# One encoder layer on one core: how the sums of squares reach memory, and when the last layer's stored products leave

## The chip, the cores and the metric

The kernel runs on one core of one Trainium2 chip, as one launch. The metric is the device time in microseconds (us) of that core, the median of several runs of the same program; lower is better. Beside the timed runs there is one profiled execution, from which all views of the trace come.

## The reference, cut to what matters

Two request groups (prompt and sample) of 2048 tokens with 1024 channels share one set of weights. For each group the layer computes, in float32:

```
h    = x * rsqrt(mean(x*x) + eps) * norm_w            # per token
proj = h @ w_in                                       # q_a k_a v_a g_a | q_b k_b v_b g_b
o_a  = windowed_gqa_sink(rope(rms(q_a)), rope(rms(k_a)), v_a) * silu(g_a)     # +-128 tokens
o_b  = neighbourhood_attn(rms(q_b), rms(k_b), v_b, rpb) * silu(g_b)           # 64-wide token grid
x    = x + concat(o_a, o_b) @ w_out
y    = x + (p @ w_ple) * sigmoid(x @ w_ple_gate)
```

Only one detail of it is touched by the first half of the change: `mean(x*x)` is needed once per token by group A, whose tiles hold 128 consecutive tokens, and again by group B, whose tiles hold 8 x 16 patches of the token grid. The second half touches how `p @ w_ple` is kept until the last line needs it.

## The kernel before, in words

Every product is split into three float32r products (high x high, high x low, low x high), so the matrix engine (PE) carries some three times the plain work. The work runs in four stages.

- **Group A**, 32 tiles of 128 tokens (16 for each of the two sequences), up to about 715 us. `proj_a(f)` projects tile f: 24 matmuls each for k and v (tile `pk`), for q (`pq`) and for the gate (`pg`). Two attention units per tile (`unit_a`, one for each key head) run between those matmuls.
- **Group B**, 64 tiles (two halves of the heads), up to about 1740 us, in the same manner (`proj_b`, `unit_b`).
- **The product p @ w_ple**, made by `ple_ahead(n)` for n = 0 to 7, eight blocks m of 6 matmuls each: PSUM tile `pple`, copied by ScalarE (ACT) into `ev` and stored by SyncE's DMA queue (SP) to `ple_d`. The first five n run beside the last units of group B, the last three alone (`tail=True`).
- **The two output products**, `product(m, mi)` into PSUM tiles `acca` and `accc`, with the operand pieces split by ACT (L1208) and VectorE (DVE, L1209).

What sets the order: all PE instructions are chained in the order in which the program emits them (`pinned`). `filler(f)` yields one projection matmul at a time, and the loop over f mixes these with the parts of the attention units at the shares of a tile that PLAN_A and PLAN_B give. A step marked `P` (keep_in_program_order) stays behind the instruction emitted before it on its own engine; unmarked ones are placed by the framework's scheduler. Every DMA that the change and its surroundings touch is issued by SP, in one queue, and runs on the same 16 DMA engines.

Buffers that matter: PSUM tag "ms" has two banks, shared by `pkt` (keys turned), `pqt` (queries turned), `po` (a unit's output, held until L741 has read it) and, in the last stage, the first two `acca`. Tag "pj" has three banks, shared by the projections, by `pple` and by later accumulators, the third and fourth `acca` among them. In SBUF, tag "s" has five buffers: in the last three `ple_ahead` they hold `ev`, so the copy of a block waits until the store of the block five before it has landed; after that they hold the results `r`.

The mean of squares of tile f is column f of `ms_a`, one number per partition, made early in the tile (L502) from the two squares of the token-major loads `stn` (L338, squared by ACT at L369). It is stored at L601 at the end of the tile. For group B `regroup(s)` lists, after the last tile of a sequence, sixteen gathers that read it back in the order of the patches (`regroup_next`, two per tile, L639) into `ms_b`.

In `ple_ahead`, `store_ple(1)` after the copy of block m issues the store of block m-1 (list `made`), so each store is queued one block late; the two extra calls `store_ple(1)` (after `drain(stream)` and after `drain(rest)`) issue the ones left over.

Of the kernel before, what the change touches and what calls it, by code (L numbers as in the profile page):

```python
# [11 lines left out]
F32 = mybir.dt.float32  # L12
# [5 lines left out]
SEQ = 2048  # L18
DM = 1024
NT = SEQ // 128  # L20
# [80 lines left out]
def emit(ctx, tc, io):  # L101
    nc = tc.nc
# [4 lines left out]
    def ptile(shape, tag, name):  # L107
        tag = PSM.get(tag, tag)
        return pp.tile(shape, F32, tag=tag, name=name, bufs=PSB[tag])
# [8 lines left out]
    ms_a = cp.tile([128, 2 * NT], F32, tag="ms_a", name="ms_a")  # L118
# [11 lines left out]
    ms_d = dram.tile([2 * SEQ], F32, tag="ms_d", name="ms_d")  # L130
# [28 lines left out]
    P = tc.keep_in_program_order  # L159
# [6 lines left out]
    def flush(key):  # L166
        pump(max((i + 1 for i, (k, _) in enumerate(jobs) if k == key), default=0))
# [72 lines left out]
    def pinned(ins):  # L240

        if last_pe:
            tc.add_manual_dep(ins.ins, last_pe.pop().name,
                              mybir.DependencyInfo(mybir.DependencyClass.NoSync, mybir.DependencyReason.DATA),
                              reason="tensor engine order")
        last_pe.append(ins.ins)
# [7 lines left out]
    def mm(out, lhsT, rhs, start, stop):  # L254
        pinned(nc.tensor.matmul(out, lhsT, rhs, start=start, stop=stop))  # L255

    def tr(out, in_, eye=ident):
        pinned(nc.tensor.transpose(out, in_, eye))  # L258
# [63 lines left out]
    ap = ab_stack.enter_context(tc.tile_pool(name="ab", bufs=1))  # L322
# [60 lines left out]
    ps = ptile([128, 512], "ms", "pwarm")  # L383
# [82 lines left out]
    for i in range(2):  # L466
        t = ap.tile([128, 2, 512], F32R, tag=f"q2{i}", name=f"q2{i}")
# [24 lines left out]
    def proj_a(f):  # L492
        s, t = divmod(f, NT)
# [68 lines left out]
        sq = ap.tile([128, 512], F32, tag="sq", name="sq", bufs=2)  # L562
# [35 lines left out]
        else:  # L598
            gate()
        held[f] = q, gs, y  # L600
        P(nc.sync.dma_start(ms_d[128 * f:128 * f + 128].rearrange("(p c) -> p c", c=1), ms))  # L601
        if t == NT - 1:
            regroup(s)
        else:
            regroup_next()
# [23 lines left out]
    def regroup(s):  # L629
        rows = ms_d.rearrange("(r k c) -> r k c", k=4, c=16)  # L630
        regroups.extend((ms_b[:, i:i + 1], rows[8 * (i // 4):8 * (i // 4) + 8, i % 4, :].rearrange("r c -> c r"))
                        for i in range(NT * s, NT * s + NT))
# [3 lines left out]
    def regroup_next():  # L636

        for dst, src in regroups[:2]:
            P(nc.sync.dma_start(dst, src))  # L639
        del regroups[:2]  # L640
# [293 lines left out]
    ple_d = [dram.tile([128, KT, TW], F32, tag=f"ple_d{n}", name=f"ple_d{n}") for n in range(len(tiles))]  # L934
    p_st, p_rs, early = {}, {}, {}

    def load_p(n):
        if n < len(tiles):
            s, u = tiles[n]
            p_st[n] = []  # L940
            for k in range(2):
                st = main.tile([128, TW], F32, tag="stage", name="p32", bufs=2)
                nc.sync.dma_start(st, io["p_t"][s][128 * k:128 * k + 128, TW * u:TW * u + TW])
                p_st[n].append(st)

    def split_p(n, later=False):

        t = p_rs[n] = main.tile([128, 2, 2, TW], F32R, tag="xr", name="p_r", bufs=2)

        def job(hi, lo, src):  # L950
            nc.scalar.copy(hi, src)
            nc.vector.tensor_tensor(out=lo, in0=src, in1=hi.bitcast(F32), op=ALU.subtract)
        for k, src in enumerate(p_st.pop(n)):
            todo = partial(job, t[:, k, 0], t[:, k, 1], src)
            if later:
                jobs.append((f"p{n}", todo))
            else:
                todo()
# [13 lines left out]
    def load_coming(n=1):  # L972

        for name, tag, key in coming[:n]:
            w = main.tile([128, 2, 512], F32R, tag=tag, name=tag, bufs=1)
            nc.sync.dma_start(w.bitcast(F32), parts_d[key])
            early[name].append(w)
        del coming[:n]

    made = []  # L980

    def store_ple(n):

        for dst, ev in made[:n]:
            nc.sync.dma_start(dst, ev)
        del made[:n]

    def ple_ahead(n, tail=False):

        load_p(n + 1)  # L990
        for m in range(KT):
            if m % 4 == 3 and (n < 3 or m == 3):
                load_coming()
            ps = ptile([128, TW], "pj", "pple")
            if m == 5 and n + 1 < len(tiles):
                split_p(n + 1)
            flush("p0")
            for k in range(2):
                w, c = early["p"][2 * (m // 4) + k], 128 * (m % 4)
                for i, (a, b) in enumerate(((0, 0), (0, 1), (1, 0))):  # L1000
                    mm(ps, w[:, a, c:c + 128], p_rs[n][:, k, b], k == 0 and i == 0, k == 1 and i == 2)
                    yield 215
            if tail:
                ev = main.tile([128, TW], F32, tag="s", name="ev", bufs=SB)
            else:
                ev = ap.tile([128, TW], F32, tag=("ev", "sq")[m // 2 % 2], name="ev", bufs=3 - m // 2 % 2)
            P(nc.scalar.copy(ev, ps))
            store_ple(1)
            made.append((ple_d[n][:, m], ev))

    qs = {}

# [4 lines left out]
    def filler(f):  # L1017

        gen = proj_a(f) if f < 2 * NT else proj_b(f)
        for n, (cost, last_one) in enumerate(gen):  # L1020
            if last_one:
                next(gen)
            elif hold[0] > 0:
                hold[0] -= 1
            elif n % step[0] == step[0] - 1:
                pump()
            yield cost

    def drain(gen, count=10 ** 9):
        for _ in range(count):  # L1030
            if next(gen, None) is None:
                return
# [16 lines left out]
    def paired(f, n):  # L1049
# [20 lines left out]
        else:  # L1070
            for name in ("a12", "a22"):
                load_early(name)
        w_b[half] = w

    stream = chain(*(paired(f, last[f]) if f in last else filler(f) for f in range(2, 6 * NT) if f - 1 not in last),
                   *(ple_ahead(n) for n in range(AHEAD)))
    drain(stream, 24)
    done = 2
# [32 lines left out]
                keys_b(*p)  # L1111
            owed = 16
    drain(stream)
    store_ple(1)


    ab_stack.close()
    with tc.tile_pool(name="c", bufs=1, reuse_waits="tile") as op:
# [171 lines left out]

        load_raw(0, 0)
        drain(ple_ahead(AHEAD, True))
        load_raw(0, 1)
        drain(ple_ahead(AHEAD + 1, True))
        for _ in range(4):
            load_x()
# [5 lines left out]
            piece(0, k)  # L1302
        load_q(0, "s2")
        drain(rest)
        store_ple(1)
        for _ in range(4):
            load_x()
        for name in ("s1", "s3", "s4"):
# [1 line left out]
        for m in range(7 * len(groups)):  # L1310
            n, i = divmod(m, 7)
# [92 lines left out]
```

## Time and profile before

| | |
|---|---|
| median of 3 runs | 2491.75 us (2488.02 to 2493.52) |
| the profiled execution | 2489.69 us, span of its instructions 2487.9 us |
| PE busy | 2459.3 us, 99% of the span |
| DVE / ACT / POOL (GpSimd) busy | 1702.9 / 1413.9 / 863.4 us |
| mean granted TensorE clock | 0.997 |
| DMA packets; under 512 B | 247140; 32400 |

How to read the views that follow. In a timeline or a group, a line names the start, the time taken, the engine, the line of the kernel, the operation, its output and input tiles, the count ("x6": six instructions merged), and in square brackets how long the engine stood idle before it and what released it. In a waits view the three numbers are total us, how often, and the longest. A line of the windows view gives, for a stretch of the span, its length, the busy time of each engine with the count of instructions, the granted clock of PE (PEclk, 1.00 is full), the busy share of the DMA engines, and GB/s. A busy PE is not PE at its peak: matmul ends are modelled, and a matmul at half clock counts as busy too.

### The profile page before, as it was taken

The page shows a single profiled execution, that of the slowest core. Times are in us where ns is not written, and L with a number is a line of the kernel's source. Part 1 is how long each engine was busy: PE and PEld are TensorE (multiplying, and loading weights), DVE is VectorE, ACT ScalarE, POOL GpSimd, SP SyncE. Part 2 cuts the span into 40 slices and gives each one's busy share as a digit, 9 for nine tenths or more (in the row PEclk, how much of TensorE's full clock was granted, in tenths as well). Part 3 has the DMA queues.
Part 4 walks back from the last instruction along what each step waited for, and adds up shares of the span by engine and source line. Part 5 has one row for each costly group of instructions (what it writes and reads, how often), then busy time and mean ns, then how long its engine had stood idle before and what let it go on. Part 6 is the DMA issues. An engine that isn't in the chain of part 4 may idle for free.

```text
span 2487.9 us, 40537 instructions
## 1 busy us (share of the span) xinstructions
PE 2459.3 (99%) x13048; PEld 2078.0 (84%) x13048; DVE 1702.9 (68%) x4210; ACT 1413.9 (57%) x3405; POOL 863.4 (35%) x1365
## 2 busy tenths in 40 slices
PE   9999999999999999999999999999999999999999
PEld 7888888888878888888788888888777888888887
DVE  6777777777765666666666666666536655687776
ACT  6777776777664665565656566666653222344443
POOL 5555555555444544544444444443100000000000
PEclk9999999999999999999999999999999999999999
DMA  7655554455374566555855566667876445756765
GB/s 204 143 111 96 98 88 102 96 92 98 82 195 137 167 190 183 169 167 184 288 171 184 177 205 210 199 198 239 295 255 233 161 169 175 267 171 219 243 227 169
DMA packets 247140, 438.87 MB, mean 176 GB/s; under 512 B 32400, under 2 KB 86800, under 8 KB 241680
## 3 DMA queue, kind: packets, MB, share of 16 engines
q1 hardware_dynamic: 246640, 436.27, 59.6%
q8 instruction: 104, 1.70, 0.3%
q14 instruction: 108, 0.88, 0.1%
q10 hardware_dynamic: 288, 0.01, 0.0%
HBM read 308.24 MB, written 133.19 MB: 177 GB/s over the span
## 4 chain that ended last, share of the span: by engine, by line
PE 91%; DMA 4%; DVE 3%; ACT 1%; issue 1%; POOL 0%; SPq 0%; ACTq 0%; DVEq 0%; POOLq 0%
PE pqk L255 14%; PE acca L1226 14%; PE pvg L255 14%; PE accc L1226 10%; PE pg L255 6%; PE pq L255 5%; PE scb L255 4%; PE ptb L258 3%; PE pob L255 3%; PE pple L255 3%; PE pk L255 3%; PE po L255 3%; PE sc L255 3%; PE pt L258 2%; DMA stn<-x_n 1%; DMA vw<-v_d 1%
## 5 line engine op out<-in xcount | busy, mean ns | idle before, releaser
L287 ACT ACTIVATE s<-s,nm 128x320 f32<-128x320 f32 (+6 forms) x512 | 294.4, 576 | 314.9 <-DVE nm L282 193.9
L255 PE MATMUL pvg<-wb,xr 128*128 128x512 f32 x1536 | 462.6, 408 | 1.3 <-DMA wb<-sp_0wb 0.6
L255 PE MATMUL pqk<-wa,xr 128*128 128x512 f32 x1536 | 442.9, 410 | 0.0
L255 PEld LDWEIGHTS pqk<-wa,xr 128*128 128x128 f32 x1536 | 266.1, 189 | 36.9
L255 PEld LDWEIGHTS pvg<-wb,xr 128*128 128x128 f32 x1536 | 266.7, 189 | 34.2 <-DMA wb<-sp_0wb 2.2
L1208 ACT CAST opd<-raw 128x512 fp32r<-128x512 f32 x224 | 131.5, 618 | 273.3 <-PE acca L1226 115.2
L356 POOL TENSOR_TENSOR xr<-stx,xr 128x512 fp32r<-128x512 f32 x188 | 241.6, 1295 | 106.3 <-ACT xr L355 84.0
L1209 DVE TENSOR_TENSOR opd<-raw,opd 128x512 fp32r<-128x512 f32 x224 | 146.4, 685 | 151.7 <-ACT opd L1208 151.7
L255 PE MATMUL pg<-wb,xr 128*128 128x512 f32 x768 | 233.5, 410 | 1.8 <-DVE vv L518 1.0
L255 PE MATMUL pq<-wa,xr 128*128 128x512 f32 x768 | 219.4, 400 | 0.0
L271 DVE CUSTOM_DVE_ANT_0 s<-scb,bias 128x288 f32<-128x288 f32 (+3 forms) x256 | 142.0, 555 | 104.6 <-PE scb L255 104.5
L137 POOL TENSOR_TENSOR yb<-vrb,power 128x8 f32<-128x8 f32 x64 | 106.5, 1664 | 236.1 <-DVE vrb L787 222.6
L1226 PE MATMUL accc<-opd,wb 128*128 128x512 f32 x768 | 176.7, 389 | 0.0
L1226 PE MATMUL acca<-opd,wa 128*128 128x512 f32 x768 | 176.6, 391 | 0.0
L1226 PE MATMUL acca<-opd,s 128*128 128x512 f32 x768 | 175.4, 389 | 0.0
L1226 PEld LDWEIGHTS acca<-opd,wa 128*128 128x128 f32 x768 | 145.1, 189 | 30.3
L1226 PEld LDWEIGHTS accc<-opd,wb 128*128 128x128 f32 x768 | 144.2, 188 | 29.9
L1226 PEld LDWEIGHTS acca<-opd,s 128*128 128x128 f32 x768 | 144.2, 188 | 29.9
L918 DVE TENSOR_TENSOR otb<-pob,otb 64x512 f32<-64x512 f32 x128 | 88.1, 689 | 112.8 <-ACT otb L917 111.2
L255 PEld LDWEIGHTS pob<-p_t,vw 128*128 128x128 f32 (+2 forms) x832 | 133.0, 189 | 27.6 <-DVE p_t L899 5.0
L255 PEld LDWEIGHTS pq<-wa,xr 128*128 128x128 f32 x768 | 135.1, 189 | 17.3
L715 DVE TENSOR_TENSOR pr<-pt,pr 128x512 fp32r<-128x512 f32 (+2 forms) x248 | 135.5, 549 | 16.5 <-ACT pr L713 13.2
(167 smaller groups left out, 5177.0 us busy)
## 6 DMA issues: line engine op xcount, KB each, us to landing
stx<-x_b SPq DMA_DIRECT2D x128, 256.0 KB
vw<-v_d SPq DMA_DIRECT2D x112, 256.0 KB
stx<-x_a SPq DMA_DIRECT2D x64, 256.0 KB
stn<-x_n SPq DMA_DIRECT2D x64, 256.0 KB
v_d<-vb SPq DMA_DIRECT2D x64, 256.0 KB
ple_d<-ev SPq DMA_DIRECT2D x64, 256.0 KB
xres<-x_r SPq DMA_DIRECT2D x64, 256.0 KB
x_d<-r SPq DMA_DIRECT2D x64, 256.0 KB
```

What stands on the lines that cost most here:

```text
L137: nc.gpsimd.tensor_tensor(out=y, in0=v, in1=power.broadcast_to([128, n]), op=ALU.pow)
L255: pinned(nc.tensor.matmul(out, lhsT, rhs, start=start, stop=stop))
L258: pinned(nc.tensor.transpose(out, in_, eye))
L271: nc.vector.tensor_tensor_reduce(out=s, in0=ps[:, :n], in1=bias, scale=1.0, scalar=-3.0e38, op0=ALU.add, op1=ALU.max, accum_out=sm["mx"][: ...
L287: ex = nc.scalar.activation(ss[i], ss[i], AF.Exp, bias=nm[:, i:i + 1], accum_out=den[:, i:i + 1])
L356: low.tensor_tensor(out=lo, in0=raw, in1=hi.bitcast(F32), op=ALU.subtract)
L715: nc.vector.tensor_tensor(out=pr[r, 1, to], in0=pt[r, c], in1=pr[r, 0, to].bitcast(F32), op=ALU.subtract)
L918: nc.vector.tensor_tensor(out=ot[a:a + 64], in0=pq[a:a + 64], in1=ot[a:a + 64], op=ALU.add)
L1208: P(nc.scalar.copy(hi, v))
L1209: P(nc.vector.tensor_tensor(out=lo, in0=v, in1=hi.bitcast(F32), op=ALU.subtract))
L1226: pinned(nc.tensor.matmul(ps, w[k][:, a, c:c + 128], o[:, b], start=i in (0, 1, 4) and k == 0 and j == 0, stop=k == 3 and j == 2, skip_gro ...
```

## The change

After it, tiles 0 to 14 and 16 to 30 store no sums. At the last tile of each sequence (t = 15, so f = 15 and f = 31) PE turns the sixteen columns of `ms_a` of that sequence into sixteen rows of 128 (PSUM tile `pms`, tag "ms"), ACT copies them into `row` (tag "sq"), and one DMA stores them as sixteen rows. The gathers of `regroup` stay as they are.

In the last three `ple_ahead` each block's store is issued right after its own copy. The two extra `store_ple(1)` calls are gone; the one store that is left over from n = 4 is issued by the call at the first block of n = 5.

```diff
@@ -598,8 +598,12 @@
         held[f] = q, gs, y
-        P(nc.sync.dma_start(ms_d[128 * f:128 * f + 128].rearrange("(p c) -> p c", c=1), ms))
         if t == NT - 1:
+            ps = ptile([128, 512], "ms", "pms")
+            tr(ps[:NT, :128], ms_a[:, NT * s:NT * s + NT])
+            row = ap.tile([128, 512], F32, tag="sq", name="row", bufs=2)
+            P(nc.scalar.copy(row[:NT, :128], ps[:NT, :128]))
+            P(nc.sync.dma_start(ms_d[s * SEQ:(s + 1) * SEQ].rearrange("(t p) -> t p", p=128), row[:NT, :128]))
             regroup(s)
         else:
             regroup_next()
@@ -1006,7 +1010,10 @@
             P(nc.scalar.copy(ev, ps))
             store_ple(1)
-            made.append((ple_d[n][:, m], ev))
+            if tail:
+                nc.sync.dma_start(ple_d[n][:, m], ev)
+            else:
+                made.append((ple_d[n][:, m], ev))
@@ -1111,7 +1118,6 @@
     drain(stream)
-    store_ple(1)
@@ -1302,7 +1308,6 @@
         drain(rest)
-        store_ple(1)
```

## The prediction

> **What bounds the kernel now.** I read the page first, then the waits of PE, then the timeline around its longest stalls, and last the DMA rate in the stretches that those led to.
>
> ```profile
> span 2487.9 us, 40537 instructions
> PE 2459.3 (99%) x13048; PEld 2078.0 (84%) x13048; DVE 1702.9 (68%) x4210; ACT 1413.9 (57%) x3405; POOL 863.4 (35%) x1365
> PE pple L255 <- ACT ev L1007: 5.7, 1, 5.7
> PE pt L258 <- DVE ot L742: 5.4, 2, 4.9
> PE pvg L255 <- DMA wb<-sp_0wb: 0.6, 2, 0.3
> ```
>
> PE is busy for 2459.3 of 2487.9 us: 28.6 us is idle, and no edit that leaves the matmuls alone can bring much more than that (plus what a slowed clock behind a stall costs). The first two rows of the waits are single stalls of 5.7 and 4.9 us, over a third of that idle time. So the question is whether the change touches one of them. It touches both.
>
> **The tail stall (the second half of the change).** Timeline around the last `ple_ahead`, SP, ACT and PE, then the chain and a windows row:
>
> ```profile
> 1853.29 3.30 SPq L1245 DMA_DIRECT2D xres<-x_r  x4
> 1856.64 0.43 SPq L1158 DMA_DIRECT2D raw<-oa_d  x1
> 1857.12 0.50 SPq L1160 DMA_DIRECT2D raw<-ob_d  x1
> 1857.72 2.05 SPq L985 DMA_DIRECT2D ple_d<-ev  x3
> 1859.82 4.80 SPq L1140 DMA_DIRECT2D s<-sums  x4
> 1866.83 6.61 SPq L985 DMA_DIRECT2D ple_d<-ev  x6
> 1853.41 0.59 ACT L1007 COPY ev<-pple 128x512 f32<-128x512 f32 x1 [0.55 <-PE pple L255]
> 1860.07 0.59 ACT L1007 COPY ev<-pple 128x512 f32<-128x512 f32 x1
> 1867.91 1.56 ACT L1007 COPY ev<-pple 128x512 f32<-128x512 f32 x3 [7.25 <-DMA ple_d<-ev]
> 1868.55 2.93 PE L255 MATMUL pple<-p_r,wa 128*128 128x512 f32 x6 [5.68 <-ACT ev L1007]
> 1871.28 12.08 PE L1226 MATMUL acca<-opd,wa 128*128 128x512 f32 x48
> L1226 PE MATMUL acca<-opd,wa 128*128 128x512 f32 x768 | 176.6, 391 | 0.0
> 1868.55:1871.48 2.93, 2.93 (x7) 2.35 (x8) 0.00 (x0) 0.93 (x2) 0.00 (x0) 0.50 1.05 401
> ```
>
> Read it backwards. PE's last six `pple` matmuls (n = 7, m = 7) waited 5.68 us for a PSUM bank: tag "pj" has three, and block 7 takes the one of block 4. Block 4's copy waited in ACT (7.25 us) for one of the five "s" buffers, the one whose store is that of the block five earlier, n = 6, m = 7. By the code that store is queued one block late, so SP reaches it only after the four residual loads and the two `raw` loads of 1 MB: it is the first of the three at 1857.72, although its copy, the one at 1853.41, was over by 1854.0. Behind 2 MB of reads it landed at about 1867.9, when the three waiting copies start.
>
> With the change that store goes out right behind its copy, ahead of the residual loads from 1853.29 and of the 2 MB. Block 4 is copied at about 1860.7, behind the copy at 1860.07, and block 7's matmuls start where PE stopped, 1868.55 - 5.68 = 1862.87. What is won: the 5.68 us, and the slow clock after it. A matmul of 512 columns takes 176.6/768 = 0.23 us; the six took 2.93 instead of 1.38, and the next 48 took 12.08 instead of 11.04, while the granted clock stood at 0.50: 2.6 us more. Together 8.3 us.
>
> The Trainium skill, in TensorE: Matmul & The Clock Gate, Part 1 (The HAM clock gate), says that about 3.4 us without work drops PE to half clock and about 3.4 us of work lifts it again. By that rule a long stall would cost 1.7 us extra where the rows here show 2.6; with 1.7 at both stalls the sum below would be 0.6 us smaller. The rows decide.
>
> What is late next in the tail: blocks 5, 6 and 7 of n = 7 now wait for the stores of blocks 0, 1 and 2, which stand behind the 2 MB as the three of 1857.72 did before, so their copies run from about 1867.9 to 1869.7. PE does not need them at once: block 7 ends at 1864.25, the first two `acca` take the "ms" banks (24 x 0.23 = 5.5 us, to 1869.8), and only the third wants block 5's bank, which is free by about 1868.5. That leaves a margin of about 1 us. Behind block 7's copy ACT starts the next operand pieces near 1870.3, and PE wants the first of them after four `acca`, at 1864.25 + 11.0 = 1875.3. SP now stands at each store until its copy is done, under 1 us for the loads behind it, the 2 MB among them; that eats some of the margins. I take 7.5 of the 8.3 us, with 0 and 8.3 as ends.
>
> **The 679 us stall (the first half).** Rows of the timeline (SP, ACT, DVE, PE), then windows:
>
> ```profile
> 662.75 0.80 SPq L601 DMA_DIRECT2D ms_d<-ms_a  x1
> 666.34 1.58 SPq L338 DMA_DIRECT2D stn<-x_n  x2
> 675.60 0.63 ACT L369 ACTIVATE stn<-stn 128x512 f32<-128x512 f32 x1 [4.92 <-DMA stn<-x_n]
> 677.72 0.86 DVE L741 TENSOR_TENSOR ot<-po,ot 64x256 f32<-64x256 f32 x2 [6.38 <-ACT ot L738]
> 679.35 1.12 PE L258 MATMUL pt<-ident,s 128*128 128x128 f32 x4 [4.88 <-DVE ot L742]
> 679.35:683.50 4.15, 4.15 (x23) 4.15 (x24) 4.03 (x11) 1.72 (x4) 1.03 (x1) 0.66 0.11 33
> 21.69 1.11 SPq L601 DMA_DIRECT2D ms_d<-ms_a  x1
> 40.66 0.59 SPq L601 DMA_DIRECT2D ms_d<-ms_a  x1
> 35.04 2.83 DMA stn<-x_n
> 43.75 9.09 DMA stn<-x_n
> 351.52 0.80 SPq L601 DMA_DIRECT2D ms_d<-ms_a  x1
> 355.11 1.58 SPq L338 DMA_DIRECT2D stn<-x_n  x2
> 365.13 0.94 SPq L338 DMA_DIRECT2D stx<-x_a  x2
> 355.00:363.50 8.50, 8.50 (x50) 7.28 (x49) 6.11 (x21) 4.92 (x16) 5.11 (x14) 1.00 0.87 51
> 365.00:368.50 3.50, 3.50 (x22) 3.04 (x22) 3.33 (x14) 1.56 (x7) 1.78 (x2) 1.00 0.47 150
> ```
>
> PE's stall of 4.88 us is released by DVE, DVE by ACT, and ACT stood 4.92 us at L369 for the `stn` load issued at 666.34. Two loads of 256 KB needed some 9 us. Elsewhere two such loads need 3: the pair of 365.13 is over by 368.5 (150 GB/s x 3.5 us is the 512 KB). In a usual tile the pair of 355.11 trickles at 51 GB/s for 8.5 us while the DMA engines count as 0.87 busy: its packets are slow, not absent. What stands ahead of the slow pairs and not of the fast ones is `ms_d<-ms_a`, 128 elements of 4 bytes each: 3.6 us before the loads of 355.11 and of 666.34, but 13.6 us before the fast ones of 365.13. The chain gives the test where the same tensor is read: `stn` took 2.83 us at 35.04, 13 us behind the store of 21.69, and 9.09 us at 43.75, 3 us behind that of 40.66. So I read the rows as: a store in 4-byte elements slows the reads of the next 8 to 10 us to a third.
>
> The Trainium skill, in DMA: Bandwidth & Descriptors, Specifications, says that a transfer under 512 B makes the DMA engine read, change and write back. It says nothing of reads that follow; by the rule alone the tiny stores cost only themselves, nobody waits for them, and this half of the change would bring nothing.
>
> Of the 32 stores 30 go, and the two left have rows of 512 B. In most tiles the trickle is hidden, since `stn` is squared a tile ahead (PE idles by nothing in 355 to 363.5). At 666.34, where the order changes towards group B, ACT needs it at 675.60 - 4.92 = 670.68; undisturbed it lands by 666.34 + 3.4 = 669.7. Won: 4.88 us, and the slow clock behind it, (1 - 0.66) x 4.15 = 1.4 us: 6.3 us, with 0 as the other end. Of the smaller waits, the 0.5 left in the `pt` row and the 0.6 of `pvg` on its weights, loaded just behind the last two stores, I take 0.8. Next late at 679 is nothing that I see; 30 issues of 0.8 us leave SP, on which nothing waits there.
>
> **What the turned rows cost.** At f = 15 and f = 31, PE order, so everything waits behind the transpose:
>
> ```profile
> 348.97 0.86 DVE L741 TENSOR_TENSOR ot<-po,ot 64x256 f32<-64x256 f32 x2 [2.17 <-ACT ot L738]
> 349.28 1.37 PE L255 MATMUL pk<-wx,xr 128*128 128x256 f32 x10
> 350.06 0.69 ACT L592 ACTIVATE gs<-pg,y 128x512 f32<-128x512 f32 x1
> 355.59 0.64 PE L255 MATMUL po<-pr,vv 128*128 128x256 f32 x4
> 357.26 0.69 DVE L315 TENSOR_TENSOR q<-pqt,q 64x512 fp32r<-64x512 f32 x1
> 713.45 0.69 ACT L592 ACTIVATE gs<-pg,y 128x512 f32<-128x512 f32 x1
> 713.55 0.60 PE L258 MATMUL pqt<-ident,q 128*128 128x128 f32 x4
> ```
>
> A transpose is 0.60/4 = 0.15 us; I take 0.2 each. At f = 15 (PE at 349.28) both "ms" banks are held, by `pqt` until L315 and by `po` until L741 ends at 349.83: PE waits 0.55 us. The row copy is behind `gs` in ACT, after 350.75; the casts behind it move by under 0.7 us, which PE's other work covers. At f = 31 one bank is free, but then `pqt` at 713.55 needs the one that `pms` holds until ACT, behind `gs` (to 714.14), has copied it, in 0.3 to 0.7 us: PE waits about 1.0. On SP the second row store stands among the weight loads for group B's first tile, and holds those behind it for its copy, up to 1 us; the first gathers wait for it as they now wait for the tile's own store. Sum 0.4 + 0.55 + 1.0, so 2.0 us lost (0.4 to 4).
>
> **Sum**: -7.5 - 6.3 - 0.8 + 2.0 = -12.6 us. The profiled execution, 2489.69, would become 2477.1; it stood 2.06 under the median, so the median becomes 2491.75 - 12.6 = 2479.2 us.
>
> **Rivals.** Four, each with what speaks for it and its time.
>
> **The tiny stores are not the cause.** The slow `stn` loads belong to `x_n`, or to the bulk stores of the same time. For it: in the usual tiles both come at the same distance, every time. Against it: 35.04 beside 43.75. Then -7.5 + 2.0: 2486.3 us. The rule quoted above from the Trainium skill (DMA: Bandwidth & Descriptors, Specifications), taken by itself, leads here too.
>
> **The tail gives its gain back.** Blocks 0 to 2 of n = 7 land later than I take, so the third `acca` waits as block 7 did, or the pieces come late. For it: the DMA engines run full there (1.05 of a stretch); the margin is 1 us. Then -7.1 + 2.0: 2486.7 us.
>
> **Slower: the banks of "ms" go round in turn.** If a new tile gets the bank after the last one and not whichever is free, the `po` of 355.59 must wait for `pqt`'s last reader, 357.26 + 0.69 = 357.95, 2.4 us, and I take the same again for `pqt` at f = 31 (an estimate, for the `po` ahead of it). With 0.55 and the transposes 5.7 us, so 2497.4 where neither gain comes, 2482.8 where both do. It decides only if the gains are under it; two-bank tiles alternate in the trace either way.
>
> **Nothing comes of either half**: 2493.8 us, the costs alone; the order of unmarked instructions changes with any edit.
>
> **How the numbers follow.** Forecast 0.60, the cause elsewhere 0.12, the tail's gain lost 0.15, banks in turn 0.05, nothing 0.08. The measurement tells 0.2%, 5.0 us, from no change, so faster means under 2486.8. The forecast lies there; of the first two rivals, which end on that line, a little over half: 0.60 + 0.07 + 0.08 = 0.75. Slower is the third, 0.05; the same is the rest, 0.20. The forecast's own bounds, -16 to -9, are 2476 to 2483; the range reaches past the two rivals at 2486.5, to 2488, and at the low end to 2473 for small waits that go with the two stalls.
>
> **What would show it.** Right: `pt` and `pple` gone from the head of PE's waits; ACT's wait at L369 near 0; the `stn` pairs at some 150 GB/s in every tile; the granted clock at 1.00 after 679 and at the start of `acca`; at the turned rows 0.5 and 1 us of PE idle. Wrong: `stn` still trickling with no 4-byte store ahead; a PE wait of several us on `acca` by ACT's `ev`; `po` waiting on L315.

## The result, and the profile after

Five runs of each kernel on the same chip: 2475.32 us after (2473.24 to 2475.44) against 2491.75 us before (2488.02 to 2494.69). The ratio is 0.9927, 95% interval 0.9913 to 0.9941: 16.4 us faster, where 12.6 had been forecast. The profiled execution went from 2489.69 to 2475.44 us, 14.25 us less.

First the page of the changed kernel, then the waits of PE (total us, how often, the longest):

```profile
span 2473.7 us, 40510 instructions
PE 2456.2 (99%) x13050; PEld 2076.4 (84%) x13050; DVE 1703.6 (69%) x4210; ACT 1413.8 (57%) x3407; POOL 864.0 (35%) x1365
q1 hardware_dynamic: 242096, 436.27, 54.4%
```

```profile
PE pob L255 <- DMA vw<-v_d: 2.9, 3, 2.4
...
PE sc L255 <- DVE pr L719: 0.8, 2, 0.6
...
PE pqt L258 <- ACT row L605: 0.5, 1, 0.5
PE pms L258 <- DVE ot L745: 0.5, 1, 0.5
```

Both single stalls that headed the list before are gone. Left at the head is a wait of group B for its values, which was there before too. New are the two rows of 0.5, both at the turned rows, and most of the 0.8 for `pr` (0.2 before).

Timeline of the changed kernel, around the turned row of f = 15, the former stall at 679, the turned row of f = 31, and the tail:

```profile
348.41 0.86 DVE L745 TENSOR_TENSOR ot<-po,ot 64x256 f32<-64x256 f32 x2 [2.17 <-ACT ot L742]
349.42 0.27 PE L258 MATMUL pms<-ident,ms_a 128*16 128x128 f32 x1 [0.48 <-DVE ot L745]
355.82 0.64 PE L255 MATMUL po<-pr,vv 128*128 128x256 f32 x4
666.56 1.59 SPq L338 DMA_DIRECT2D stn<-x_n  x2
670.82 0.62 ACT L369 ACTIVATE stn<-stn 128x512 f32<-128x512 f32 x1
674.48 0.60 PE L258 MATMUL pt<-ident,s 128*128 128x128 f32 x4
676.00 0.45 PE L255 MATMUL sc<-ks_a,q 128*128 128x320 f32 x2
677.38 0.56 PE L255 MATMUL sc<-ks_a,q 128*128 128x320 f32 x2 [0.58 <-DVE pr L719]
678.74 0.46 PE L255 MATMUL sc<-ks_a,q 128*128 128x320 f32 x2
708.38 0.69 ACT L592 ACTIVATE gs<-pg,y 128x512 f32<-128x512 f32 x1
708.97 0.24 ACT L605 COPY row<-pms 16x128 f32<-16x128 f32 x1
709.26 0.66 PE L258 MATMUL pqt<-ident,q 128*128 128x128 f32 x4 [0.52 <-ACT row L605]
725.61 0.45 PE L255 MATMUL sc<-ks_a,q 128*128 128x320 f32 x2
1847.60 0.59 ACT L1011 COPY ev<-pple 128x512 f32<-128x512 f32 x1 [0.59 <-PE pple L255]
1848.21 0.32 SPq L1014 DMA_DIRECT2D ple_d<-ev  x1
1848.62 1.83 SPq L1251 DMA_DIRECT2D xres<-x_r  x4
1858.23 11.04 PE L1232 MATMUL acca<-opd,wa 128*128 128x512 f32 x48
1861.85 0.59 ACT L1011 COPY ev<-pple 128x512 f32<-128x512 f32 x1 [6.53 <-DMA ple_d<-ev]
```

The store of n = 6, m = 7 (1848.21) now leaves right behind its copy of 1847.60, ahead of the residual loads of 1848.62. ACT finds `stn` landed at 670.82 and waits for nothing. Block 5's copy (1861.85) still waits 6.53 us for a store behind the 2 MB, as forecast, but ends at 1862.44, and the third `acca` wants its bank only at 1858.23 + 24 x 0.23 = 1863.75: 1.3 us to spare.

In a usual tile of group A, in the stretch in which the DMA engines were 0.87 busy at 51 GB/s, they are now 0.26 busy at 80 (the row's last two numbers):

```profile
355.00:363.50 8.50, 8.50 (x51) 7.28 (x50) 6.11 (x23) 4.76 (x16) 4.41 (x12) 1.00 0.26 80
```

Now the sum along time. A row of before and the same instruction's row of after give the shift at that point. These pairs use the rows above, those of the prediction, and the last of five rows of before that were not shown yet; the other four serve further below:

```profile
60.13 0.66 PE L258 MATMUL pt<-ident,s 128*128 128x128 f32 x4 [0.54 <-DVE ot L742]
682.18 0.47 PE L255 MATMUL sc<-ks_a,q 128*128 128x320 f32 x2
683.78 0.45 PE L255 MATMUL sc<-ks_a,q 128*128 128x320 f32 x2
721.77 0.50 PE L255 MATMUL pvg<-wb,xr 128*128 128x512 f32 x1 [0.25 <-DMA wb<-sp_0wb]
731.35 0.45 PE L255 MATMUL sc<-ks_a,q 128*128 128x320 f32 x2
```

| up to | the same instruction, before and after | shift | this step | forecast |
|---|---|---|---|---|
| f = 15 | `ot` 348.97, 348.41 | -0.56 | -0.6 | (small waits) |
| behind its row | `po` 355.59, 355.82 | +0.23 | +0.8 | +0.75 |
| behind 679 | `gs` 713.45, 708.38 | -5.07 | -5.3 | -6.3 |
| behind the row of f = 31 | `pqt` 713.55, 709.26 | -4.29 | +0.8 | +1.2 |
| behind group B's first weights | `sc` 731.35, 725.61 | -5.74 | -1.45 | -0.8 with the first line |
| start of the last blocks | `ev` 1853.41, 1847.60 | -5.81 | -0.1 | 0 |
| end of the first four `acca` | 1883.36, 1869.27 | -14.09 | -8.3 | -7.5 |

### The profile page after: what moved, and what is told of

Its sections match the earlier page's. It is cut to its first block, busy times and chain, and to the rows that moved or that the text cites. A ratio compares the mean times of both kernels' runs of the same rounds, so it can differ in the third digit from the quotient of the medians.

```text
span 2473.7 us, 40510 instructions
## 1 busy us (share of the span) xinstructions
PE 2456.2 (99%) x13050; PEld 2076.4 (84%) x13050; DVE 1703.6 (69%) x4210; ACT 1413.8 (57%) x3407; POOL 864.0 (35%) x1365
## 4 chain that ended last, share of the span: by engine, by line
PE 94%; DVE 2%; DMA 1%; ACT 1%; issue 0%; POOL 0%; SPq 0%; ACTq 0%; DVEq 0%
PE pqk L255 14%; PE pvg L255 14%; PE acca L1232 14%; PE accc L1232 10%; PE pq L255 6%; PE pg L255 6%; PE scb L255 4%; PE ptb L258 4%; PE pob L255 3%; PE pple L255 3%; PE pk L255 3%; PE po L255 3%; PE sc L255 3%; PE pt L258 2%; DVE pr L719 1%; PE pktb L258 1%
```

## The experiments

Each time is a median of five runs or more. Each ratio is to the kernel before, timed beside it; its median went from 2491.75 to 2493.28 us over these series.

**The two halves apart.** First half alone, then second half alone.

```diff
# e1_rows: turned rows as in the change; the stores of the last layers as before
# e2_tail: the last layers' stores as in the change; the old store of the sums
```

> The first half of the change alone: rows for the 4-byte stores, last layers' results stored one block late as before. If the two halves are independent, the 4.9 us wait of PE near 679 goes and the 5.7 us wait of pple stays: the profiled span falls from 2487.9 to about 2482 (5.3 us at 679, 0.8 at the start and 1.6 at the weight loads behind 713 won, 1.7 lost at the two turned rows). Rival: the whole gain of this half hangs on the other half or the slow loads are not due to these stores; then the 4.9 us wait stays and the span is 2488 to 2490.

> The second half alone: results of the last layers stored at once, the 4-byte stores kept. Forecast: the 4.9 us wait near 679 stays with its slow clock, the 5.7 us wait of pple goes with its slow clock: span 2487.9 - 8.3 = 2479.6. Rival: the tail's gain needs the other half (DMA less busy): then PE waits for pple or for the third acca by several us and the span stays above 2484.

First half alone 2482.16 us (ratio 0.9967, 0.9955 to 0.9978), second half alone 2484.11 us (0.9975, 0.9966 to 0.9984), the kernel before, beside them, 2491.77. That is 9.6 and 7.7 us, together 17.3, against 16.4 for both at once: within the intervals the halves add. The waits of PE, of the first half alone and then of the second:

```profile
PE pple L255 <- ACT ev L1011: 5.2, 1, 5.2
```

```profile
PE pt L258 <- DVE ot L742: 6.2, 1, 6.2
PE pvg L255 <- DMA wb<-sp_0wb: 2.3, 3, 1.0
```

Each half leaves the other's stall in place. The second half alone came out 1.9 us over its expected span (2481.5 for 2479.6), and its rows point at the first half's place: the waits that it does not touch were larger in this execution (6.2 us for the 4.9 of before at 679, 2.3 for 0.6 at the weights). What the small stores cost varies from run to run.

**Is it the small stores, and what of them?** To the changed kernel a store to a tensor that nobody reads is added at the old place, in every tile unless said otherwise:

```diff
+        P(nc.sync.dma_start(mx_d[128 * f:128 * f + 128], SRC))
# e3_tiny_back:   SRC = ms              128 elements of 4 B, packed
# e4_wide_back:   SRC = ident           128 rows of 512 B
# e5_one_tiny:    SRC = ms, f == 29 only
# e6_b64_back:    SRC = ident[:, :16]   128 rows of 64 B, packed
# e9_tiny_spread: SRC = ms, into mx_d[..., 0:1] of rows of 64 B
# e10_b16_back:   SRC = ident[:, :4]    128 elements of 16 B, packed
```

> The changed kernel plus, at the place of the old store, a store of the same 128 elements of 4 bytes to a tensor that nobody reads. If 4-byte elements slow the reads behind them: the stn pairs take 8 to 9 us again, the DMA engines' busy share in 200:345 goes from 0.29 back to about 0.5, PE waits 4 to 5 us near 679 again, and the span is 2473.7 + 5.3 + 1.6 + 0.8 = about 2481. Rival 1, the slow loads came from something else (the reader of the sums, the order of the queue): nothing waits for this store, span 2474, share 0.29.

> The changed kernel plus, at the same place, a store of 128 rows of 512 bytes (a constant matrix) to a tensor that nobody reads: as many descriptors and as many issues as the old store, 128 times the bytes. If it is the size of the elements: stn loads stay at about 3 us a pair, busy share in 200:345 about 0.30, no wait near 679, span 2474. Rival 2, any store of 128 pieces just ahead of the loads slows them, or its issue on SP does: wait of 4 to 5 us near 679, span about 2481.

Measured: 2485.79 us (0.9972, 0.9964 to 0.9981) with the tiny stores back, 2475.92 (0.9943, 0.9930 to 0.9955) with the wide ones. Windows with PE alone (length, PE busy, granted clock, DMA share, GB/s), the tiny stores first, then the wide:

```profile
200.00:345.00 145.00, 145.00 (x879) 1.00 0.53 95
650.00:690.00 40.00, 34.09 (x203) 0.91 0.27 69
```

```profile
200.00:345.00 145.00, 145.00 (x881) 1.00 0.30 96
650.00:690.00 40.00, 38.36 (x237) 1.00 0.38 126
```

At the same GB/s the DMA engines are busy for 0.53 of the time with the tiny stores and 0.30 without, and the stall at 679 is back (5.9 us in the waits). Nobody waits for the added store or reads it, so rival 1, that the slow loads came from elsewhere, is out; the wide ones have as many issues and descriptors, so rival 2 is out too. The profiled execution with the tiny stores came out some 5 us over the expected span (2486.6 for 2481), by a longer stall (5.9 us in place of 4.9) and later weights (1.4 us in PE's waits, 0.6 before).

> The changed kernel plus one single store of 128 elements of 4 bytes, in tile f = 29 only (the one ahead of the loads at 666). If each such store slows just the reads of the next 8 to 10 us: PE waits 4.9 to 6.2 us near 679 (with the slow clock behind it 5.3 to 7.5 us in all), the busy share in 200:345 stays at 0.29, nothing else moves, span 2479 to 2481. Rival: the slowing builds up over many such stores; then one of them leaves no wait near 679 and the span is 2474.

One tiny store in one tile: 2479.42 us (0.9948, 0.9935 to 0.9960), 4.1 over the changed kernel, and its chain and waits show where:

```profile
666.70 6.50 DMA stn<-x_n
```

```profile
PE pt L259 <- DVE ot L749: 3.5, 1, 3.5
```

A single store is enough for a stall, so a long build-up is not needed. But the wait is 3.5 and the load took 6.50, under the bracket that I gave and under the 9.07 to 9.31 of the kernels with a store in every tile (the one of before took 9.18). Whether earlier stores add to a later one, or one execution is just milder, stays open.

> The changed kernel plus, in each tile, a store of 128 rows of 64 bytes. If all elements under 512 bytes act as the 4-byte ones: busy share in 200:345 about 0.5, wait of 4.9 to 6.2 us near 679, span 2481 to 2487. If only the smallest do: share 0.30, no wait, span 2474. In between: share 0.3 to 0.5 and a wait of 1 to 4 us.

> The changed kernel plus, in each tile, the 128 elements of 4 bytes again, but each at the start of its own 64 bytes of the unread tensor (the addresses of the 64-byte store, 4 bytes at each). If the size of an element is what counts: share in 200:345 about 0.5, wait of 3.5 to 6.2 us near 679, span 2479 to 2487. If it is that 128 elements fall into the same 512 bytes: share 0.30, no such wait, span 2474 to 2476.

> The changed kernel plus, in each tile, a store of 128 elements of 16 bytes, one behind the other (2 KB). If only whole 64-byte pieces escape: share in 200:345 of 0.35 to 0.5, a wait of 1 to 6 us near 679, span 2477 to 2487. If the slowing is one of 4-byte elements alone: share 0.30, no wait, span 2474 to 2476.

Measured 2474.46 (0.9931, 0.9918 to 0.9943) with 64 bytes, 2474.11 (0.9925, 0.9911 to 0.9938) with 4 bytes spread, 2475.61 (0.9929, 0.9917 to 0.9942) with 16 bytes packed: none costs anything that can be told. The DMA share in 200:345 is 0.30, 0.29 and 0.31, and no wait at 679 comes back. The sharpest pair is the queue's row (packets, MB, share of 16 engines) of the packed 4-byte stores and of the spread ones:

```profile
q1 hardware_dynamic: 246704, 436.29, 60.0%
```

```profile
q1 hardware_dynamic: 246704, 436.29, 54.1%
```

The same packets and the same bytes, from the same source at the same place; only the addresses differ, and 5.9% of the DMA engines' span goes with them. So the trickle is not a matter of the elements' size alone, as the prediction had it, nor of packing alone, since 16 bytes packed do no harm: it takes 4-byte elements packed next to each other, 128 of them in 512 bytes. Where between 4 and 16 bytes, or between a spacing of 4 and of 64, it ends was not tried. The Trainium skill, in DMA: Bandwidth & Descriptors, Specifications, puts a bound at 512 B per transfer, below which there is a read-modify-write. The runs do not bear out a cost to other transfers by that bound: rows of 64 bytes and spread elements of 4 lie under it and slow nothing here. What happens inside the memory with packed 4-byte writes, no view shows.

**Which late store.** The first half, and one store of the second:

```diff
+            if n == AHEAD + 1 and m == KT - 1:
+                nc.sync.dma_start(ple_d[n][:, m], ev)
+            else:
+                made.append((ple_d[n][:, m], ev))
```

> The first half of the change, and of the second half one store only: that of n = 6, m = 7 goes out at once, the 15 others of these two layers and those of the layer before stay one block late. Theory: that store alone holds the buffer that pple waits for, so the 5.2 us wait of the first half alone goes with its slow clock, span 2480.7 - 7 = 2473.7 as with the whole change. Rival: the stores of n = 7 that stand late behind the two 1 MB loads stop PE next (third acca); then a wait of several us remains near 1860 and the span is over 2476.

In the profiled execution the theory holds: span 2473.4, and PE runs from `pple` into `acca` without a break.

```profile
1847.84 8.78 PE L255 MATMUL pple<-p_r,wa 128*128 128x512 f32 x38
1856.45 11.04 PE L1233 MATMUL acca<-opd,wa 128*128 128x512 f32 x48
1864.43 0.59 ACT L1011 COPY ev<-pple 128x512 f32<-128x512 f32 x1 [2.67 <-DMA ple_d<-ev]
1876.91 3.02 PE L1233 MATMUL accc<-opd,wb 128*128 128x512 f32 x12 [0.82 <-DVE r L1277]
```

But the last copy is later than in the whole change (it starts 8.0 us behind the start of `acca` here, at 1864.43; there some 5.0, the second of the two from 1862.65), a wait of 0.82 shows on `accc`, and the five runs lie at 2475.20 to 2480.77 with a median of 2477.57 (0.9943, 0.9930 to 0.9957). That one store is the cause of the stall; whether the 15 others are worth up to 2 us more in some runs is not settled, since the intervals overlap.

**Cheaper ways to the first half.**

```diff
# e8_sc_bank
-            ps = ptile([128, 512], "ms", "pms")
+            ps = ptile([128, 512], "sc", "pms")
# e11_pad64: no turned rows; the sum written 16 times, stored per tile as 64-byte rows
+        ms_w = ap.tile([128, 16], F32, tag="ms_w", name="ms_w", bufs=3)
+        P(nc.vector.tensor_scalar(out=ms_w, in0=ssq[:, 10:11].broadcast_to([128, 16]), ...
+        P(nc.sync.dma_start(ms_d[128 * f:128 * f + 128], ms_w))
# e12_spread: no turned rows; the old store, each element to its own 64 bytes
+        P(nc.sync.dma_start(ms_d[128 * f:128 * f + 128, 0:1], ms))
```

> The changed kernel, the transposed sums in a PSUM bank of tag sc (three banks) in place of ms (two). If the 0.48 us (at 349, by DVE ot) and 0.52 us (pqt at 709, by ACT row) that PE waits at the turned rows are for the bank alone: both go, span 2473.7 - 1.0 = 2472.7. Rival: the next scores or transposes of that tag wait for the row copy behind gs in place of them, 0.3 to 0.7 us each, span 2473.3 to 2474.

2474.54 us (0.9929, 0.9916 to 0.9941), span 2472.3. Both waits for the bank are gone, but behind f = 31 PE now waits 0.66 us for DVE:

```profile
349.21 0.27 PE L258 MATMUL pms<-ident,ms_a 128*16 128x128 f32 x1
709.34 0.60 PE L258 MATMUL pqt<-ident,q 128*128 128x128 f32 x4
716.29 0.53 PE L255 MATMUL sc<-ks_a,q 128*128 128x320 f32 x2 [0.66 <-DVE pr L719]
```

So 0.5 us is won at f = 15, but at 675.16 PE waits 0.40 us for DVE's `ot`, where the changed kernel waits for nothing (674.48), and the gain at f = 31 is handed on to the next wait. By the times it is not to be told from the change.

> The changed kernel without the turned rows: the sum of squares is written 16 times over a 64-byte row in SBUF and stored per tile as 128 rows of 64 bytes, and the gathers read the first element of each row. No transpose, bank or row copy. If the 64-byte store costs the reads nothing when it carries the sums too: the 0.75 us at f = 15 and the 0.9 us at f = 31 go, no wait near 679 comes back, span 2473.7 - 1.7 = 2472. Rival: the store now depends on DVE and its rows are read again, and reads slow as before: span over 2478.

2492.82 us (0.9998, 0.9990 to 1.0007): my estimate failed, but not by the stated rival. The DMA share in 200:345 is 0.29, so the trickle is gone; PE waits on DVE instead, 27 times, and its weight loads stand 20.0 us in the same wait (2.1 in the changed kernel). Waits of PE, then the timeline of the first tile (DVE) and of a usual one (POOL and DVE):

```profile
PE sc L254 <- DVE mx L270: 9.7, 27, 0.6
```

```profile
20.36 0.23 DVE L503 TENSOR_SCALAR ms_w<-ssq 128x16 f32<-128x16 f32 x1
223.24 2.53 POOL L355 TENSOR_TENSOR xr<-stx,xr 128x512 fp32r<-128x512 f32 x2
223.51 1.05 DVE L503 TENSOR_SCALAR ms_w<-ssq 128x16 f32<-128x16 f32 x1
```

The operation of 16 columns takes 0.23 us at the start, when POOL is idle, and 1.05 in a usual tile (median 1085 ns), ending at 224.56, when the first of POOL's two operations ends, if both took the same time (223.24 + 2.53/2 = 224.5). The one-column operation it replaced takes 203 to 206 ns in all 32 tiles of the changed kernel, beside the same POOL work. The Trainium skill, in SBUF — State Buffer, Who interferes with whom, says that a `tensor_scalar` whose operands meet the conditions of a two-port mode can take a port pair that DVE and GpSimd hold one at a time, each for a whole instruction; these rows agree with it, though no view shows the mode. The shift against the changed kernel, by the starts of this operation and of the one it replaced, grows to 19 us over group A (20.36 for 20.0 in the first tile, 699.6 for 680.0 in the last).

> The second half of the change, and for the first half one thing only: the old store of 128 elements of 4 bytes per tile stays (no transpose, no row), but each element goes to the start of its own 64 bytes of ms_d, and the gathers read there. If the slowing came of 128 small writes into the same 512 bytes: no wait of several us near 679, share in 200:345 of 0.29, and without the 0.75 and 0.9 us of the turned rows the span is 2473.7 - 1.65 = 2472. Rival: with a tensor that is read afterwards the small writes slow the loads as before, span over 2478; or the gathers at a stride of 64 bytes come late for group B: a wait behind 713 that the changed kernel hasn't.

2475.49 us (0.9927, 0.9913 to 0.9940), span 2474.0. No stall of several us at 679, the share is 0.30, and neither late gathers nor late weights hold PE behind 713. The turned rows' cost is gone but does not show at the end: half a us returns at 674 (the 0.5 for `ot`), and later waits differ by one or two us in both directions.

```profile
PE pob L255 <- DVE p_t L899: 2.1, 2, 1.6
PE accc L1228 <- DVE r L1272: 0.7, 1, 0.7
PE pt L258 <- DVE ot L742: 0.5, 1, 0.5
```

So a change of the address alone brings what the transposes, the bank and the row copy bring. No version tried is faster than the changed kernel by more than the measurement tells.

## Why the prediction was right, point by point

- **The tail stall.** Right in mechanism and in order: the store of n = 6, m = 7 was the one to move (shown by the one-store kernel), and the stores behind the 2 MB stayed late without stopping PE. Mis-sized: I took 7.5 of 8.3 for fear of the third `acca`. The margin that I called about 1 us was 1.3, as its own figures give (1869.8 less 1868.5), and all 8.3 came.
- **The 679 stall.** Right that the sums' stores made the `stn` loads slow and that nothing of x_n's own did (shown by putting them back and by the single store). Wrong in what about them: I named the 4-byte element; the runs show that it takes such elements packed, and that 4 bytes spread or 16 bytes packed do no harm. The forecast held because the rows that replaced them are harmless by either reading. Mis-sized: 5.3 for 6.3. The whole 6.3 had come by the first `sc` behind the stall (682.18 against 676.00, a shift of -6.18 from +0.23 at f = 15), but by the fourth 1.1 was given back (683.78 against 678.74): at the full clock, where before it was 0.66 for the same work, PE comes to the second `sc` ahead of DVE and waits for its `pr`, 0.58 us in the row of 677.38. "Next late at 679 is nothing that I see" was the step that failed.
- **Small waits.** Forecast 0.8, measured 0.6 at tile 2 (the 0.54 of 60.13) and 1.45 at group B's first weights, 2.05 in all. I had counted only the waits of the matmuls, 0.6 us at the weights (0.25 of them at 721.77). The weight loads of PE, which stand in a row of their own, waited longer for the same loads, and in the changed kernel they have no such row:

```profile
PEld pvg L255 <- DMA wb<-sp_0wb: 2.2, 5, 0.7
```

- **The turned rows.** Forecast 2.0, measured 1.6. The bank waits came where said, 0.48 us by `ot` for the 0.55 forecast and 0.52 by `row` for 1.0.
- **The rivals.** "The tiny stores are not the cause" is out by the stores put back, "the tail gives its gain back" by the second half alone, "the banks go round in turn" by the trace of after, in which no `po` waits on L315, and "nothing comes of either half" by the result itself.
- **From 14.25 to 16.4.** The profiled executions differ by 2489.69 - 2475.44 = 14.25 us, 1.65 more than the forecast; 1.0 too much at 679 stands against too little in the tail (0.8), the small waits (1.2) and the rows (0.4), so part of the closeness is luck. The rest of the measured gain is the step from the profile to the median: the profiled execution of before stood 2.06 under its median and that of after 0.12 over its own, and 14.25 + 2.06 + 0.12 = 16.43. I had carried the gain over as if every run of before paid the same. So the median, 2475.32, lies 0.7 us under the forecast's own bounds (2476 to 2483), in the strip down to 2473 that I had added for small waits; of the 3.8 us by which the gain was missed, 2.2 are this step and not small waits. The stall at 679 was 4.9 us in that execution and 6.2 and 5.9 in the two other kernels with packed stores in every tile, so that profile was likely a mild one; with three executions this is a reading and not shown.

## What to carry to other kernels

When loads are slow while the DMA engines count as busy, look at what was stored shortly before them: here packed 4-byte elements cost the next loads, not the storer, and giving each element its own 64 bytes was enough. In the tail a store queued behind 2 MB of loads landed some 10 us later, and the wait appeared where its buffer came round again. Before taking a profile's stall at face value as the gain in the median, see whether the profiled execution stands at its kernel's median.

## What the runs showed of the hardware that was not expected

128 packed 4-byte writes slow the loads of 256 KB issued some 3 us behind them from 2.8 to 9 us (6.5 where there was a single such store), and the same writes 64 bytes apart do not: 60.0% against 54.1% of the DMA engines' span for the same 246704 packets. A DVE operation of 16 columns took 1.05 us beside POOL and 0.23 without it, while one of a single column took 0.20 in both cases.
